# NSA heads: two heads to one float32 transpose, the high and low parts split behind it, and the rotation on VectorE ahead of 1 / rms

## The chip, the cores and the metric

The kernel runs on one core of one Trainium2 chip. The metric is the device time of one execution in microseconds, the median of several runs. The engines are called by the names of the profile: PE (TensorE matmul), PEld (its weight loads), DVE (VectorE), ACT (ScalarE), POOL (GpSimd), SP (SyncE, which only issues transfers).

## The reference, cut to what matters

One layer: a gated feed-forward half step, a mixing part, a second feed-forward half step, and a gated embedding. The change lies in the mixing part, in its native-sparse-attention (NSA) heads. For 512 tokens and 8 query heads, 2 key/value heads of 64 columns:

```
u = a @ w_in                                   # a: normed tokens, 512 x 1024
q_a   = partial_rope(rmsnorm(split_heads(qa, 8), q_norm_nsa), cos, sin)
kc_tok = partial_rope(split_heads(kc, 2), cos, sin)     # compressed keys, no norm
k_slc = partial_rope(rmsnorm(split_heads(ksl, 2), k_norm_slc), cos, sin)
k_win = partial_rope(rmsnorm(split_heads(kwn, 2), k_norm_win), cos, sin)
o_a = nsa_attention(q_a, k_cmp, v_cmp, k_slc, v_slc, k_win, v_win, gates)
```

`rmsnorm` is over the 64 columns of one head, with a gain per column. `partial_rope` rotates the first 16 columns of a head by the token's angle. The rotation and the factor 1 / rms (one number for each token and head) can change places, since a rotation is linear; the gain must stand ahead of the rotation.

## The kernel before, in words

All matrix products are made of float32 split in two parts, hi (the value rounded to the type of TensorE's fast pass, fp32r) and lo (the rest): three passes hi·hi, hi·lo, lo·hi. For the scores of attention a head's 64 columns of hi and 64 of lo stand above each other in the 128 partitions, so that two passes do all.

The program isn't written in the order in which it runs. Every operation is recorded by `Plan.record` (so every instruction has line 306), and `Plan.issue` lists them engine by engine with costs of its own (`Plan.cost`), taking at each step the operation that could start first. So a change in one place moves instructions on all engines. Several streams are woven together by `weave`; the first stage of the mixing part weaves `kv_project` and `q_project(0)` with the compression of keys and values, the second (`c0 n00 | q1`) the attention of the first four heads with `q_project(1)`.

The mixing part lies at 309 to 688 us of the span, the two feed-forward parts on either side of it. What the change touches, each once for each of the four tiles of 128 tokens:

- `c_done` (the projection "c"): scales the columns of the compressed keys and values (tile `u`, a `w` buffer), rotates the two key heads in place with `rope` on POOL, transposes four heads, copies them to `T2`.
- `kv_done` (the projection "v"): four key heads (selected and window, two each). ACT squares, DVE sums (`TENSOR_REDUCE`), POOL makes 1 / rms (`rstd`: two instructions, the tiles `s` and `mhalf`), DVE multiplies by it and then by the gain, POOL rotates (`rope`), ACT and DVE split into hi and lo side by side (`split_heads`, the tile `hl`), PE transposes each head's 128 columns (hi and lo), and ACT or DVE copies three times for each kind into `B`.
- `q_done` (the projections "q0" and "q1"): the same for four query heads, with `head_norm`, and one ACT copy for each two heads (`qT`) into `A`.

`rope` is four instructions: the product with the cosines, two with the sines, and the sum, on 64 columns (four heads) or 32 (two heads). The transposes take PSUM tiles named `gub`; matrix products take `acc` or `gub`. The tiles `st`, `x`, `hi`, `lo` are weights as loaded and as split; each split is an ACT cast to `hi` and a DVE subtraction to `lo`.

Of the kernel before, what the change touches and what calls it, by code (L numbers as in the profile page):

```python
# [7 lines left out]
F32 = mybir.dt.float32  # L8
F32R = mybir.dt.float32r
AF = mybir.ActivationFunctionType  # L10
ALU = mybir.AluOpType
AX = mybir.AxisListType
PSUM = bass.MemoryType.PSUM

P = 128
# [293 lines left out]
class Layer:  # L309
# [443 lines left out]

    def head_norm(self, E, src, dst, gain):
# [31 lines left out]
    def qT(self, hl, heads, dst, t):  # L786

        nc = self.nc
        ps = self.gub()
        for i, hd in enumerate(heads):  # L790
            nc.tensor.transpose(ps[:, i * P:(i + 1) * P], self.parts(hl, hd, 0), self.ident)
        nc.scalar.copy(dst[:, :, t * P:(t + 1) * P], ps[:, :2 * P].rearrange("p (a c) -> p a c", a=2))
# [185 lines left out]
    def cmp_attention(self, A, t, g, o):  # L978
# [4 lines left out]
        for hd in range(4):  # L983
            a = A[hd // 2][:, hd % 2, t * P:(t + 1) * P]
            nc.tensor.matmul(pv[:, hd], lhsT=a, rhs=self.kcT[:, :, g * 32:g * 32 + 32], start=True, stop=True)
# [84 lines left out]
    def mix(self, xT, rs_in, o_nsa, o_fox, nsa_out):  # L1070
# [4 lines left out]
        def c_done(t, ps):  # L1075
# [6 lines left out]
            self.rope(G, uv[:, 0:2], t, 2)  # L1082
# [13 lines left out]
        def kv_project():  # L1096
# [4 lines left out]
            def kv_done(t, ps):  # L1101
                u = self.w2()
                nc.scalar.mul(u, ps, rs_in[t])
                uv = u.rearrange("p (a s h d) -> p a s h d", a=2, s=2, h=2)
                for kind in range(2):
                    self.vsplit(uv[:, kind, 1], Vt[kind], t)
                xn = self.w2()[:, :256]
                x4 = xn.rearrange("p (a h d) -> p a h d", a=2, h=2)
                sq, ss = self.w2()[:, :256], self.small(4)
                nc.scalar.activation(sq.rearrange("p (a h d) -> p a h d", a=2, h=2), uv[:, :, 0], AF.Square)  # L1110
                V.tensor_reduce(ss, sq.rearrange("p (n d) -> p n d", n=4), axis=AX.X, op=ALU.add)
                r = self.rstd(ss, 64, 4).rearrange("p (a h) -> p a h", a=2)
                V.tensor_tensor(x4, uv[:, :, 0], r[:, :, :, None].to_broadcast([P, 2, 2, 64]), ALU.mult)
                V.tensor_tensor(x4, x4, self.gkv[:, :, None, :].to_broadcast([P, 2, 2, 64]), ALU.mult)
                xn = xn.rearrange("p (n d) -> p n d", n=4)
                self.rope(G, xn, t, 4)
                hl = self.split_heads(xn, 4, 2)
                cols = slice(t * P, (t + 1) * P)
                for kind in range(2):
                    tp = self.gub()  # L1120
                    for i in range(2):
                        nc.tensor.transpose(tp[:, i * P:(i + 1) * P], self.parts(hl, 2 * kind + i, 0), self.ident)
                    k = tp[:, :256].rearrange("p (a c) -> p a c", a=2)
                    copy = nc.scalar.copy if (t + kind) % 2 else V.tensor_copy
                    copy(B[kind][0][:, :, cols], k)
                    copy(B[kind][1][0:64, :, cols], k[64:128])
                    copy(B[kind][1][64:128, :, cols], k[0:64])
# [4 lines left out]
        def q_project(g):  # L1132
            A[g] = [self.k4((P, 2, 512), F32R) for _ in range(2)]

            def q_done(t, ps):
# [3 lines left out]
                self.head_norm(V, u, xn, self.gq[:, None, :].to_broadcast([P, 4, 64]))  # L1139
                self.rope(G, xn, t, 4)  # L1140
                hl = self.split_heads(xn, 4, 2)
                for i in range(2):
                    self.qT(hl, (2 * i, 2 * i + 1), A[g][i], t)
# [6 lines left out]
        def nsa_pair(g, a):  # L1150
            for kind in range(2):
# [10 lines left out]
                run = lambda par: self.unit([(A[g][a][:, par], B[kind][i][:, g]) for i in range(2)], Vt[kind][:, g],  # L1162
# [392 lines left out]
```

## Time and profile before

| what | value |
|---|---|
| median of 3 runs | 1085.66 us (1085.31 to 1086.53) |
| the profiled execution: its time | 1086.66 us |
| the profiled execution: its span | 1084.8 us |
| PE busy | 1068.4 us (98%), 6721 matmuls |
| DVE busy | 768.4 us (71%), 1320 instructions |
| ACT busy | 580.2 us (53%) |
| POOL busy | 184.2 us (17%) |
| granted TensorE clock | 1.000 in the mean |
| chain that ended last | PE 86%; DVE 4%; ACT 3%; POOL 3%; DMA 2% |

The span is the time from the first to the last instruction; the execution's own time is 1.9 us longer. A busy engine is one that has an instruction under way; matmuls overlap one another, so PE's busy time tells where PE had something, not what it could have done.

### The profile page before, as it was taken

The numbers are of one execution on the slowest core, as the hardware profiler recorded it, in microseconds if no ns is written. First come the engines' busy times: TensorE is split into PE (matmuls) and PEld (weight loads), VectorE is DVE, ScalarE is ACT, GpSimd is POOL, SyncE is SP. The second block draws the span as 40 slices with busy tenths as digits, with TensorE's granted clock in tenths as the row PEclk, the third lists the DMA queues.
The fourth block names the chain that finished last, engine by engine and source line by source line (L and its number), as shares of the span: only waits on it lengthen the run. The fifth ranks groups of instructions, "written<-read, shape, count | busy, mean of one in ns | idle before, by whom it ended". The sixth has DMA issues, their size and how long they took to land.

```text
span 1084.8 us, 17688 instructions
## 1 busy us (share of the span) xinstructions
PE 1068.4 (98%) x6721; PEld 962.8 (89%) x6721; DVE 768.4 (71%) x1320; ACT 580.2 (53%) x1116; POOL 184.2 (17%) x313
## 2 busy tenths in 40 slices
PE   9999999999999999999999999999999999999998
PEld 6789899988997878999999888889989998899887
DVE  5886378744774777989889786977537784487473
ACT  5544145522543768988888864645315552255352
POOL 0010000000000246554344610310000000000000
PEclk9999999999999999999999999999999999999999
DMA  8396356643444622302102241686535674333421
GB/s 280 125 232 200 97 136 184 189 130 100 118 110 131 216 70 73 86 7 60 43 18 75 76 158 52 220 222 170 173 97 145 185 185 130 103 109 120 153 109 66
DMA packets 76532, 139.79 MB, mean 129 GB/s; under 512 B 13744, under 2 KB 33712, under 8 KB 76192
## 3 DMA queue, kind: packets, MB, share of 16 engines
q1 hardware_dynamic: 71376, 120.76, 34.4%
q0 software_dynamic: 4928, 17.89, 9.4%
q8 instruction: 53, 0.87, 0.3%
q14 instruction: 31, 0.25, 0.1%
q10 hardware_dynamic: 144, 0.02, 0.0%
HBM read 132.23 MB, written 6.42 MB: 128 GB/s over the span
## 4 chain that ended last, share of the span: by engine, by line
PE 86%; DVE 4%; ACT 3%; POOL 3%; DMA 2%; issue 2%; SPq 0%; ACTq 0%; POOLq 0%; DVEq 0%
PE acc L306 53%; PE gub L306 33%; DVE k L306 1%; POOL s L306 1%; DVE lo L306 1%; ACT w L306 1%; DMA st<-in_quarters 1%; DMA st<-in_first 1%; POOL r L306 1%; ACT k L306 1%; POOL w L306 1%; DVE w L306 1%; DMA gq<-in_q_norm_nsa 1%; ACT hi L306 1%; SPq L306 0%
## 5 line engine op out<-in xcount | busy, mean ns | idle before, releaser
L306 PE MATMUL acc<-hi,k 128*128 128x512 f32 (+1 forms) x832 | 262.7, 389 | 1.5 <-ACT k L306 0.9
L306 ACT CAST hi<-st 128x1024 fp32r<-128x1024 f32 (+4 forms) x150 | 148.5, 991 | 179.7 <-PE acc L306 93.2
L306 DVE TENSOR_TENSOR lo<-st,hi 128x1024 fp32r<-128x1024 f32 (+4 forms) x150 | 172.2, 1150 | 65.6 <-ACT hi L306 65.2
L306 PE MATMUL acc<-hi,x 128*128 128x384 f32 (+3 forms) x720 | 199.5, 349 | 0.3 <-ACT hi L306 0.3
L306 PEld LDWEIGHTS acc<-hi,k 128*128 128x128 f32 x832 | 155.9, 188 | 32.6 <-ACT k L306 1.8
L306 PE MATMUL acc<-lo,k 128*128 128x512 f32 (+1 forms) x432 | 163.9, 383 | 0.6 <-DVE lo L306 0.6
L306 ACT CAST hi<-pt 128x1024 fp32r<-128x1024 f32 x68 | 71.4, 1049 | 159.1 <-PE acc L306 90.3
L306 PE MATMUL gub<-x,hi 128*128 128x256 f32 x816 | 147.5, 282 | 0.0
L306 PE MATMUL acc<-x,hi 128*128 128x256 f32 x816 | 147.3, 282 | 0.0
L306 DVE TENSOR_TENSOR lo<-pt,hi 128x1024 fp32r<-128x1024 f32 x68 | 83.2, 1223 | 79.6 <-ACT hi L306 79.6
L306 PE MATMUL gub<-k,hi 128*128 128x512 f32 (+1 forms) x560 | 138.6, 338 | 0.0
L306 PEld LDWEIGHTS acc<-hi,x 128*128 128x128 f32 x720 | 127.2, 189 | 11.0 <-ACT hi L306 0.4
L306 PE MATMUL acc<-lo,x 128*128 128x384 f32 (+3 forms) x360 | 125.0, 348 | 1.7 <-DVE lo L306 1.7
L306 PEld LDWEIGHTS gub<-x,hi 128*128 128x128 f32 x816 | 126.2, 189 | 0.5
L306 PEld LDWEIGHTS acc<-x,hi 128*128 128x128 f32 x816 | 125.7, 189 | 0.0
L306 PE MATMUL gub<-x,lo 128*128 128x256 f32 x408 | 115.3, 283 | 0.0
L306 PE MATMUL acc<-x,lo 128*128 128x256 f32 x408 | 115.3, 283 | 0.0
L306 POOL DMA_DIRECT2D pt<-in_quarters x34 | 29.9, 880 | 476.3 <-DMA pt<-in_quarters 284.8
L306 PEld LDWEIGHTS gub<-k,hi 128*128 128x128 f32 x560 | 96.3, 190 | 12.2 <-ACT hi L306 1.2
L306 PE MATMUL gub<-k,lo 128*128 128x512 f32 (+1 forms) x280 | 94.6, 338 | 0.4 <-DVE lo L306 0.4
L306 PEld LDWEIGHTS acc<-lo,k 128*128 128x128 f32 (+1 forms) x432 | 79.4, 184 | 15.7 <-DVE lo L306 0.9
L306 PEld LDWEIGHTS gub<-x,lo 128*128 128x128 f32 x408 | 76.9, 189 | 0.0
(163 smaller groups left out, 1716.0 us busy)
## 6 DMA issues: line engine op xcount, KB each, us to landing
st<-in_quarters SPq DMA_DIRECT2D x51, 512.0 KB, 3.5
st<-in_ffn_wd SPq DMA_DIRECT2D x44, 512.0 KB, 4.4
pt<-in_quarters SPq DMA_DIRECT2D x34, 512.0 KB, 4.5
pt<-in_quarters POOLq DMA_DIRECT2D x34, 512.0 KB, 6.9
st<-in_quarters SPq DMA_DIRECT2D x32, 256.0 KB, 4.9
st<-in_w_in SPq DMA_DIRECT2D x48, 128.0 KB, 2.3
st<-in_first SPq DMA_DIRECT2D x16, 256.0 KB, 4.0
st<-in_w_in SPq DMA_DIRECT2D x8, 512.0 KB
```

What stands on the lines that cost most here:

```text
L306: getattr(getattr(self.nc, op.eng), m)(*a, **k)
```

## The change

Four things are done at once, in `c_done`, `kv_done` and `q_done`:

- `turned_norm`: the gain comes first, then the rotation, on DVE, and 1 / rms is the last factor. The rotation so stands beside POOL's `rstd` and not behind it.
- `turned`: two heads of 64 float32 columns go into one transpose, so two transposes make a tile of four heads, where four made it before.
- The split into hi and lo is made on the way out of PSUM: ACT copies 64 partitions to hi, DVE subtracts it from the same 64 partitions and writes lo to the other 64.
- `c_done`'s rotation is made by DVE too.

The tiles `A` and `B` are held by other indices (`A[g][par]` for the even or odd heads, `B[g]` for the key/value head); the products that read them are as many and as large.

```diff
+    def turned_norm(self, src, dst, gain, t):
+        V = self.nc.vector
+        d4 = dst.rearrange("p (a h) d -> p a h d", a=2)
+        sq, ss = self.w2()[:, :256], self.small(4)
+        self.nc.scalar.activation(sq.rearrange("p (a h d) -> p a h d", a=2, h=2), src, AF.Square)
+        V.tensor_tensor(d4, src, gain, ALU.mult)
+        V.tensor_reduce(ss, sq.rearrange("p (n d) -> p n d", n=4), axis=AX.X, op=ALU.add)
+        self.rope(V, dst, t, 4)
+        r = self.rstd(ss, 64, 4)
+        V.tensor_tensor(dst, dst, r[:, :, None].to_broadcast([P, 4, 64]), ALU.mult)
...
+    def turned(self, x):
         ps = self.gub()
-        for i, hd in enumerate(heads):
-            nc.tensor.transpose(ps[:, i * P:(i + 1) * P], self.parts(hl, hd, 0), self.ident)
-        nc.scalar.copy(dst[:, :, t * P:(t + 1) * P], ps[:, :2 * P].rearrange("p (a c) -> p a c", a=2))
+        for i in range(2):
+            self.nc.tensor.transpose(ps[:, i * P:(i + 1) * P], x[:, 2 * i:2 * i + 2].rearrange("p a d -> p (a d)"),
+                                     self.ident)
+        return ps[:, :2 * P].rearrange("p (a c) -> p a c", a=2)
+
+    def qT(self, x, dst, t):
+        pv = self.turned(x)
+        for par in range(2):
+            r, o = slice(64 * par, 64 * par + 64), slice(64 - 64 * par, 128 - 64 * par)
+            d = dst[par][:, :, t * P:(t + 1) * P]
+            self.nc.scalar.copy(d[r], pv[r])
+            self.nc.vector.tensor_sub(d[o], pv[r], d[r].bitcast(F32))
@@ c_done @@
-            self.rope(G, uv[:, 0:2], t, 2)
+            self.rope(V, uv[:, 0:2], t, 2)
@@ kv_done @@
-                V.tensor_reduce(ss, sq.rearrange("p (n d) -> p n d", n=4), axis=AX.X, op=ALU.add)
-                r = self.rstd(ss, 64, 4).rearrange("p (a h) -> p a h", a=2)
-                V.tensor_tensor(x4, uv[:, :, 0], r[:, :, :, None].to_broadcast([P, 2, 2, 64]), ALU.mult)
-                V.tensor_tensor(x4, x4, self.gkv[:, :, None, :].to_broadcast([P, 2, 2, 64]), ALU.mult)
-                self.rope(G, xn, t, 4)
-                hl = self.split_heads(xn, 4, 2)
+                self.turned_norm(uv[:, :, 0], xn, self.gkv[:, :, None, :].to_broadcast([P, 2, 2, 64]), t)
+                pv = self.turned(xn)
-                for kind in range(2):
-                    tp = self.gub()
-                    for i in range(2):
-                        nc.tensor.transpose(tp[:, i * P:(i + 1) * P], self.parts(hl, 2 * kind + i, 0), self.ident)
-                    k = tp[:, :256].rearrange("p (a c) -> p a c", a=2)
-                    copy = nc.scalar.copy if (t + kind) % 2 else V.tensor_copy
-                    copy(B[kind][0][:, :, cols], k)
-                    copy(B[kind][1][0:64, :, cols], k[64:128])
-                    copy(B[kind][1][64:128, :, cols], k[0:64])
+                for g in range(2):
+                    r, o = slice(64 * g, 64 * g + 64), slice(64 - 64 * g, 128 - 64 * g)
+                    k = pv[r]
+                    nc.scalar.copy(B[g][0][r, :, cols], k)
+                    V.tensor_sub(B[g][0][o, :, cols], k, B[g][0][r, :, cols].bitcast(F32))
+                    nc.scalar.copy(B[g][1][o, :, cols], k)
+                    V.tensor_sub(B[g][1][r, :, cols], k, B[g][0][r, :, cols].bitcast(F32))
@@ q_done @@
-                self.head_norm(V, u, xn, self.gq[:, None, :].to_broadcast([P, 4, 64]))
-                self.rope(G, xn, t, 4)
-                hl = self.split_heads(xn, 4, 2)
-                for i in range(2):
-                    self.qT(hl, (2 * i, 2 * i + 1), A[g][i], t)
+                self.turned_norm(u.rearrange("p (a h) d -> p a h d", a=2), xn,
+                                 self.gq[:, None, None, :].to_broadcast([P, 2, 2, 64]), t)
+                self.qT(xn, A[g], t)
```

Where the listing puts the instructions, at three places.

PE, in the projection "v", the transposes of the first tile's key heads (`hl` before, `w_641` now, between the matmuls of the second tile). Before:

```order
L306 MATMUL acc<-hi,x_540 128x512
L306 MATMUL acc<-hi,x_538 128x512
L306 MATMUL acc<-lo,x_538 128x512
L306 MATMUL acc<-hi,x_540 128x512
L306 MATMUL acc<-hi,x_538 128x512
L306 MATMUL acc<-lo,x_538 128x512
L306 MATMUL gub<-ident,hl 128x128 x4
L306 MATMUL acc<-hi,x_540 128x512
L306 MATMUL acc<-hi,x_539 128x512
```

PE, the same place in the change:

```order
L306 MATMUL acc<-hi,x_538 128x512
L306 MATMUL acc<-lo,x_538 128x512
L306 MATMUL acc<-hi,x_540 128x512
L306 MATMUL gub<-ident,w_641 128x128 x2
L306 MATMUL acc<-hi,x_538 128x512
L306 MATMUL acc<-lo,x_538 128x512
L306 MATMUL acc<-hi,x_540 128x512
L306 MATMUL acc<-hi,x_538 128x512
L306 MATMUL acc<-lo,x_538 128x512
```

Four transposes became two, and they stand five matmuls of 512 columns earlier (row 1960 of the engine's list, where it was 1965).

POOL, where the query tiles of the first group are normed (`w_714`, `w_728`, `w_739` are the first three tiles before; `s_742`, `s_755` are 1 / rms of the third and fourth). Before:

```order
L306 TENSOR_TENSOR r_718<-w_714,cos 128x64
L306 TENSOR_TENSOR r_719<-w_714,sin 128x4x8 x2
L306 TENSOR_TENSOR w_714<-r_718,r_719 128x4x16
L306 TENSOR_SCALAR s_742<-s_741 128x4
L306 TENSOR_TENSOR s_742<-s_742,mhalf 128x4
L306 TENSOR_TENSOR r_732<-w_728,cos 128x64
L306 TENSOR_TENSOR r_733<-w_728,sin 128x4x8 x2
L306 MEMSET k_773 128x1024
L306 TENSOR_TENSOR w_728<-r_732,r_733 128x4x16
L306 TENSOR_SCALAR s_755<-s_754 128x4
L306 TENSOR_TENSOR r_743<-w_739,cos 128x64
L306 TENSOR_TENSOR r_744<-w_739,sin 128x4x8 x2
```

POOL, the same place in the change (`s_723`, `s_732`, `s_743` are 1 / rms of the second, third and fourth tile):

```order
L306 MEMSET k_757 128x1024
L306 TENSOR_SCALAR s_723<-s_720 128x4
L306 TENSOR_TENSOR s_723<-s_723,mhalf 128x4
L306 TENSOR_SCALAR s_732<-s_729 128x4
L306 TENSOR_TENSOR s_732<-s_732,mhalf 128x4
L306 TENSOR_SCALAR s_743<-s_740 128x4
L306 TENSOR_TENSOR s_743<-s_743,mhalf 128x4
L306 TENSOR_TENSOR pt<-pt 128x8 x3
```

POOL's rotations are gone from between the tiles' 1 / rms.

DVE, where the weights of the projection "q0" are split (`lo<-st`), beside the last key tiles (`w_667` is the third tile before, `w_663` now). Before:

```order
L306 TENSOR_TENSOR lo<-x_626,hi 128x1024
L306 TENSOR_REDUCE s_669<-w_668 128x4
L306 TENSOR_TENSOR lo<-x_627,hi 128x1024 x2
L306 TENSOR_TENSOR w_667<-w_666,s_670 128x256
L306 TENSOR_TENSOR lo<-st,hi 128x1024
L306 TENSOR_TENSOR w_667<-w_667,gkv 128x256
```

DVE, the same place in the change:

```order
L306 TENSOR_TENSOR r_667<-w_663,sin 128x4x8 x2
L306 TENSOR_TENSOR w_663<-r_666,r_667 128x4x16
L306 TENSOR_TENSOR lo<-x_626,hi 128x1024 x2
L306 TENSOR_TENSOR k_613<-gub,k_612 64x2x128
L306 TENSOR_TENSOR lo<-x_627,hi 128x1024
L306 TENSOR_REDUCE s_665<-w_664 128x4
L306 TENSOR_TENSOR lo<-x_627,hi 128x1024
L306 TENSOR_TENSOR lo<-st,hi 128x1024
L306 TENSOR_TENSOR w_663<-w_663,s_668 128x256
```

The product with 1 / rms (`w_663<-w_663,s_668`), which waits for POOL, now stands behind the split of the weights and not ahead of it; the rotation and a subtraction out of PSUM stand ahead.

Counted over the whole program, PE has 24 matmuls fewer (the transposes), DVE 72 instructions more (64 of them the rotations), ACT 8 fewer, and POOL 64 fewer.

## Rows read from the trace of the kernel before

**Rows 1.** Busy time of each engine by stretch of the mixing part.
```profile
core 0: us, PE busy (x) PEld busy (x) DVE busy (x) ACT busy (x) POOL busy (x), PEclk, DMA share, GB/s
370.00:450.00 80.00, 74.53 (x510) 66.40 (x510) 65.12 (x166) 62.50 (x152) 44.01 (x90) 1.00 0.25 72
450.00:490.00 40.00, 40.00 (x276) 37.72 (x275) 34.94 (x113) 33.79 (x102) 19.15 (x35) 1.00 0.17 42
490.00:610.00 120.00, 119.22 (x782) 110.99 (x781) 105.94 (x302) 102.98 (x291) 53.27 (x78) 1.00 0.17 45
```
**Rows 2.** Chain that ended last, 385 to 407 us: start, us, what.
```profile
385.38 0.57 POOL s L306
386.02 1.17 POOL s L306
387.21 0.44 DVE w L306
387.67 0.44 DVE w L306
388.18 0.81 POOL r L306 x3
389.06 0.33 POOL w L306
389.41 0.41 ACT hl L306
389.85 0.44 DVE hl L306
...
406.57 1.24 POOL w L306
```
**Rows 3.** Timeline of PE: start, us, instruction, idle time before and releaser.
```profile
376.93 0.63 PE L306 MATMUL gub<-ident,w 128*64 128x128 f32 x4 [0.44 <-POOL w L306]
...
390.33 0.66 PE L306 MATMUL gub<-ident,hl 128*128 128x128 f32 x4 [1.14 <-DVE hl L306]
...
405.33 0.38 PE L306 MATMUL acc<-lo,x 128*128 128x256 f32 x1 [1.10 <-DVE lo L306]
...
412.89 0.45 PE L306 MATMUL acc<-lo,k 128*64 128x256 f32 x2 [0.56 <-DVE lo L306]
...
427.70 0.66 PE L306 MATMUL gub<-ident,hl 128*128 128x128 f32 x4 [0.39 <-DVE hl L306]
```
**Rows 4.** Timeline of PE around one tile's four transposes, 395 to 397 us.
```profile
395.47 0.40 PE L306 MATMUL acc<-lo,x 128*128 128x512 f32 x1
395.70 0.39 PE L306 MATMUL acc<-hi,x 128*128 128x512 f32 x1
395.94 0.60 PE L306 MATMUL gub<-ident,hl 128*128 128x128 f32 x4
396.29 0.48 PE L306 MATMUL acc<-hi,x 128*128 128x512 f32 x1
396.61 0.39 PE L306 MATMUL acc<-lo,x 128*128 128x512 f32 x1
```
**Rows 5.** POOL's groups, 360 to 490 us: count, busy us, mean ns, idle before.
```profile
L306 POOL TENSOR_TENSOR r<-w,cos 128x64 f32<-128x64 f32 x12 | 6.4, 530 | 8.0 <-DVE w L306 7.9
L306 POOL TENSOR_TENSOR r<-w,sin 128x32 f32<-128x32 f32 x24 | 6.3, 283 | 0.0
L306 POOL TENSOR_TENSOR w<-r,r 128x64 f32<-128x64 f32 x12 | 5.6, 468 | 0.8
```
**Rows 6.** DVE's group of the split, 366 to 490 us, columns as above.
```profile
L306 DVE TENSOR_TENSOR hl<-w,hl 128x256 fp32r<-128x256 f32 x14 | 5.9, 424 | 4.8 <-ACT hl L306 4.6
```
**Rows 7.** Timeline of DVE, columns as in the timeline of PE.
```profile
390.80 1.29 DVE L306 CAST k<-gub 128x256 fp32r<-128x256 f32 x3 [0.20 <-PE gub L306]
...
403.71 0.42 DVE L306 TENSOR_TENSOR w<-w,s 128x256 f32<-128x256 f32 x1 [0.91 <-POOL s L306]
404.05 1.22 DVE L306 TENSOR_TENSOR lo<-st,hi 128x1024 fp32r<-128x1024 f32 x1
...
427.56 0.17 DVE L306 TENSOR_SCALAR w<-ch 128x32 f32<-128x32 f32 x1
427.64 0.17 DVE L306 TENSOR_SCALAR w<-pt 128x32 f32<-128x32 f32 x1
```
**Rows 8.** ACT's group of the split, 366 to 490 us.
```profile
L306 ACT CAST hl<-w 128x256 fp32r<-128x256 f32 x14 | 5.8, 412 | 4.7 <-POOL w L306 4.7
```

More of the change, by code (lines that the diff above doesn't have):

```diff
@@ L784, in parts @@
         return hl[:, hd, i:i + 2].rearrange("p a d -> p (a d)").bitcast(F32)
-    def qT(self, hl, heads, dst, t):
-        nc = self.nc
+    def turned(self, x):
         ps = self.gub()
-        for i, hd in enumerate(heads):
-            nc.tensor.transpose(ps[:, i * P:(i + 1) * P], self.parts(hl, hd, 0), self.ident)
-        nc.scalar.copy(dst[:, :, t * P:(t + 1) * P], ps[:, :2 * P].rearrange("p (a c) -> p a c", a=2))
+        for i in range(2):
[9 more added lines that the diff above has]
+            self.nc.vector.tensor_sub(d[o], pv[r], d[r].bitcast(F32))
     def vsplit(self, src, dst, t):
@@ L983, in cmp_attention @@
         for hd in range(4):
-            a = A[hd // 2][:, hd % 2, t * P:(t + 1) * P]
+            a = A[hd % 2][:, hd // 2, t * P:(t + 1) * P]
             nc.tensor.matmul(pv[:, hd], lhsT=a, rhs=self.kcT[:, :, g * 32:g * 32 + 32], start=True, stop=True)
@@ L1106, in kv_done @@
                     self.vsplit(uv[:, kind, 1], Vt[kind], t)
[L1107 to L1110, printed above, removed]
-                V.tensor_reduce(ss, sq.rearrange("p (n d) -> p n d", n=4), axis=AX.X, op=ALU.add)
-                r = self.rstd(ss, 64, 4).rearrange("p (a h) -> p a h", a=2)
-                V.tensor_tensor(x4, uv[:, :, 0], r[:, :, :, None].to_broadcast([P, 2, 2, 64]), ALU.mult)
-                V.tensor_tensor(x4, x4, self.gkv[:, :, None, :].to_broadcast([P, 2, 2, 64]), ALU.mult)
-                xn = xn.rearrange("p (n d) -> p n d", n=4)
-                self.rope(G, xn, t, 4)
-                hl = self.split_heads(xn, 4, 2)
-                cols = slice(t * P, (t + 1) * P)
-                for kind in range(2):
-                    tp = self.gub()
-                    for i in range(2):
-                        nc.tensor.transpose(tp[:, i * P:(i + 1) * P], self.parts(hl, 2 * kind + i, 0), self.ident)
-                    k = tp[:, :256].rearrange("p (a c) -> p a c", a=2)
-                    copy = nc.scalar.copy if (t + kind) % 2 else V.tensor_copy
-                    copy(B[kind][0][:, :, cols], k)
-                    copy(B[kind][1][0:64, :, cols], k[64:128])
-                    copy(B[kind][1][64:128, :, cols], k[0:64])
+                xn = self.w2()[:, :256].rearrange("p (n d) -> p n d", n=4)
+                self.turned_norm(uv[:, :, 0], xn, self.gkv[:, :, None, :].to_broadcast([P, 2, 2, 64]), t)
+                pv = self.turned(xn)
+                cols = slice(t * P, (t + 1) * P)
+                for g in range(2):
[5 more added lines that the diff above has]
+                    V.tensor_sub(B[g][1][r, :, cols], k, B[g][0][r, :, cols].bitcast(F32))
             yield from self.project(xT, [(768, 512)], kv_done, "v")
@@ L1161, in write @@
                                     tmp.rearrange("p (t c) -> p t c", t=NT), ALU.add)
-                run = lambda par: self.unit([(A[g][a][:, par], B[kind][i][:, g]) for i in range(2)], Vt[kind][:, g],
+                run = lambda par: self.unit([(A[g][par][:, a], B[g][i][:, kind]) for i in range(2)], Vt[kind][:, g],
                                             rs, par)
```

## The prediction

> **What bounds the kernel now.** I read the page first: PE is busy nearly all of the span, and the chain that ended last is PE's for 86% of it. Then I cut the mixing part into stretches, because the change lies in the first two [rows 1]. From 370 to 450 us, where the key heads and the first four query heads are projected and normed, PE is busy 74.53 of 80 us: it waits for 5.47 us. From 450 to 490 us, where the other query heads are made beside the first attention, PE is busy all the time and DVE 34.94 of 40 us. So in the second stretch PE's work itself sets the time, and in the first PE's work and a chain through the other engines in turn.
>
> The chain of one key tile shows what that chain is [rows 2]. POOL makes 1 / rms from 385.38 to 387.19 us, DVE multiplies twice, POOL rotates from 388.18 to 389.39, ACT splits off hi, DVE lo, and PE's transposes start at 390.33 [rows 3]. Between the end of POOL's 1 / rms and the transposes lie 3.1 us. PE waited 1.14 us for the last link, 0.44 us for a rotation in `c_done`, 0.39 us for the split of a query tile; and twice, 1.10 and 0.56 us, for DVE's split of weights (`lo`) [rows 3]. These five are 3.6 of the 5.47 us; the rest is in small pieces.
>
> **PE's own work.** Twelve tiles (four of keys, eight of queries) lose two transposes each, 24 in all. Price: from the matmul at 395.70 to the one at 396.61 there pass 0.91 us, in which two matmuls of 512 columns and four transposes start [rows 4]. A matmul of 512 columns takes 0.23 us start to start (395.47 to 395.70). So four transposes take 0.91 - 0.46 = 0.45 us, one 0.11, and 24 take 2.6 us. Eight of the 24 (0.9 us) lie in the second group's projection, where PE never waits; the other 16 (1.8 us) lie where PE also waits, so they count in full only if the chain gets shorter too. The matmuls that read `A` and `B` are the same in number and size, and cost the same.
>
> **The chain.** With the change 1 / rms is followed by one product (0.44 us) and the transposes. The second product, from 387.67 to 388.11 us, and what stands from there to 390.33, the rotation and both splits, fall out of it: 0.44 + 2.22 = 2.66 us for each tile. The rotation on DVE must fit beside POOL's 1.81 us of 1 / rms; by the price below it does. The first tile's transposes stand five matmuls earlier in PE's list, which takes 5 x 0.23 = 1.2 us of the 2.66 back; 1.5 us is left, over the wait of 1.14, so I let that wait go. I let go the 0.44 (POOL's rotation is not there any more, and the listing sets those transposes ten matmuls later) and the 0.39. Of the waits for weights I take 0.5 of 1.66 us away: the split that PE waits for at 405.33 started at 404.05 behind a product that had waited 0.91 us for POOL [rows 7]; that product now stands behind the split. Together 2.5 us less of waiting.
>
> **DVE, which pays.** The rotations: no row has one on DVE. From above: each instruction starts when the one ahead has ended. 32 columns last 0.17 us and 256 columns 0.42 [rows 7]; in between by the line, 64 columns 0.21 and 16 columns 0.15; so 0.21 + 0.17 + 0.17 + 0.21 = 0.76 us for four heads and 0.64 for two. From below: they start as soon as DVE takes them, 0.08 us apart at 32 columns (427.56, 427.64) and 0.34 at 256 (403.71, 404.05), so 0.12 at 64 and 0.06 at 16; 0.40 and 0.28 us. I take 0.6 and 0.5, between the two, since the three products don't wait for each other and the sum does. Twelve and four of them: 9.2 us (5.9 to 11.7). The evacuations: 32 subtractions out of PSUM come, twelve copies out of PSUM and twelve splits go. Three such copies took 1.29 us, 0.43 each [rows 7], a split 0.42 [rows 6]: 13.8 - 5.2 - 5.0 = 3.6 us. DVE so gains 12.8 us of work (9.5 to 15.3): 2.0 in `c_done`, 2.5 with the keys, 4.1 with each group of queries. The stretch to 450 us has 14.9 us in which DVE is idle and takes 8.6 of it; the stretch to 490 us has 5.1 us and takes 4.1 [rows 1]. It fits, but in the second stretch DVE is then busy 39 of 40 us, and its instructions stand in one line with the softmax. For that I set 1.0 us of new waiting for PE, between nothing (all of it fits) and 4.1 us (every added microsecond is passed on).
>
> A rule of the Trainium skill (VectorE: DVE Perf Modes, section "Two Vector instructions with no wait between them") speaks against the change: an instruction whose input or output starts in another group of 32 partitions than the last one in the same memory is held until all earlier ones have finished. The copies at 390.80, which go to the other half of the partitions, bear it out: 0.43 us each, where the product at 403.71 gave way after 0.34. By the rule each of the 32 subtractions also holds what follows it, 0.09 us more each, so 2.9 us more of DVE work than the sum has; with the crowding grown in proportion, 1.2 for 1.0 us, the time would be 1081.8.
>
> **ACT and POOL.** ACT loses twelve splits of 0.41 us [rows 8], 4.9 us, and gets a few narrow copies for wide ones; it was busy 62.5 of 80 us and on the path only within the chain counted above, so this is worth nothing more. POOL loses twelve rotations of 0.53 + 2 x 0.28 + 0.47 = 1.56 us [rows 5], 18.7 us, and those of `c_done`. It was busy 44 of 80 us, so as work that is worth nothing; as delay it is, because the sum of one rotation took 0.33 us at 389.06 and 1.24 us at 406.57 [rows 2], and POOL's 1 / rms stands in one line with it. I leave that in the rival of the larger gain. No transfer is added or moved past another; after 490 us nothing is changed but the places in the list.
>
> **Sum.** -2.6 (transposes) - 2.5 (waits gone) + 1.0 (DVE crowded) = -4.1 us. The profiled execution took 1086.66 us and would take 1082.6; it lies 1.0 us over the median of the runs shown, which stands for what will be measured: 1085.66 - 4.1 = **1081.6 us**. The likeliest case reaches from 1079.4 (no crowding, and the rest of the waits for weights, 1.2 us, gone too) to 1083.4 (2.8 us of crowding).
>
> **Rivals.**
> *DVE becomes the bound (slower).* The place is 404 to 490 us, the two query projections, where softmax, splits of weights and the new subtractions share DVE. If half of the 12.8 us that DVE gains is passed on to PE, that is +6.4 - 2.6 = +3.8 us: 1089.5. It decides from 2.6 + 2.5 = 5.1 us passed on. For it: 87% busy DVE in the second stretch already, 88% in the third. Against it: DVE's idle time in the first stretch is in part waits that the change takes away (4.6 us before the splits [rows 6]).
> *The transposes were covered.* If PE goes on waiting in the first stretch, for weights and other tiles, the 16 transposes there save nothing, and only 8 x 0.11 = 0.9 us is left: 1084.8, no change. For it: the second and third longest waits are for weights [rows 3], which DVE now makes behind more work. Against it: PE is busy 93% there, so most transposes did take time.
> *All the first stretch's waiting goes.* With POOL free of rotations and each query tile 2.7 us sooner, the attention can fill what is left: 5.47 + 2.6 = 8.1 us less: 1077.6. For it: ACT stood idle 4.7 us for POOL's rotations ahead of the splits [rows 8]. Against it: waits for transferred and split weights have nothing to do with the change.
> A listing that comes out worse elsewhere, by a new wait of some 1 us as those in [rows 3], is part of each case's width.
>
> **How the numbers follow.** A measurement of this kernel can tell about 0.2%, 2.2 us, from no change: below 1083.5 is faster, above 1087.8 slower. Chances: the forecast 0.48, all waits gone 0.15, covered 0.20, DVE the bound 0.17. So faster 0.48 + 0.15 = 0.63, same 0.20, slower 0.17. The range holds all but the slower case: 1077 to 1087.
>
> **What would show it.** Right: PE's transposes in the projections "v", "q0", "q1" two to a tile, no wait of PE for a split of heads, DVE some 10 to 15 us busier up to 490 us, PE idle 2 to 4 us in 370 to 450. Wrong: PE waiting for DVE's `lo` or for the softmax's tiles for over 5 us up to 490 us (then DVE is the bound); PE idle still over 5 us before 450 (covered); rotations on DVE over 0.8 us each.

## The result, and the profile after

The changed kernel takes 1092.65 us (median of 4 runs, 1091.36 to 1094.81); the kernel before, run beside it, 1085.49 us (1084.64 to 1086.53). The ratio is 1.0069, with an interval of 1.0057 to 1.0081: the change makes the kernel 7 us slower, where 4.1 us less was forecast. The profiled execution took 1092.93 us with a span of 1091.2 us.

The first part of the page after, with the busy time of each engine:

```profile
span 1091.2 us, 17622 instructions
PE 1070.9 (98%) x6697; PEld 963.7 (88%) x6697; DVE 780.4 (72%) x1392; ACT 579.7 (53%) x1108; POOL 161.1 (15%) x249
```

PE's 24 instructions are gone, and DVE's added work is 780.4 - 768.4 = 12.0 us, where 12.8 was forecast. But PE is busy 2.5 us longer, not 2.6 us less. The view by stretch says why (the columns are those of [rows 1]; after the five busy times comes the granted clock):

```profile
370.00:450.00 80.00, 70.42 (x461) 62.73 (x460) 67.01 (x196) 57.24 (x130) 27.34 (x40) 0.96 0.25 72
450.00:490.00 40.00, 38.89 (x255) 34.75 (x253) 38.99 (x128) 30.46 (x91) 13.29 (x24) 1.00 0.17 41
...
32.00:36.00 4.00, 4.00 (x12) 3.10 (x12) 4.00 (x7) 3.03 (x5) 0.00 (x0) 0.58 0.85 257
...
390.00:394.00 4.00, 4.00 (x12) 3.13 (x11) 3.20 (x11) 1.45 (x4) 1.21 (x2) 0.57 0.01 4
...
430.00:436.00 6.00, 4.14 (x23) 3.94 (x23) 5.78 (x18) 2.28 (x7) 1.92 (x4) 0.72 0.00 0
...
431.86:436.00 4.14, 4.14 (x23) 3.94 (x23) 3.98 (x13) 1.54 (x5) 1.92 (x4) 0.66 0.00 0
```

In 370 to 450 us PE now stands idle 9.58 us, where it was 5.47 [rows 1], and the granted clock is 0.96, where it was 1.00. The short stretches show where: from 390 to 394 us and from 430 to 436 us the clock lies part of the time at the lower of its two levels, 1.2 GHz for 2.4. PE is busy all through the first, and from 431.86 us on in the second, so (1 - 0.57) x 4 + (1 - 0.66) x 4.14 = 3.1 us of work at full speed are lost there, and 1.7 us by the same fall at 32 to 36 us, far ahead of the change.

So the 6.4 us between the two spans are: half speed +4.8 us, idle time of PE +3.9 us (1091.2 - 1070.9 = 20.3, for 1084.8 - 1068.4 = 16.4), and PE's work -2.3 us (1070.9 - 4.8 = 1066.1, for 1068.4). Two spans can be set beside each other only roughly. PE's list is the same in all kernels of this document up to its 2253rd matmul, and their profiles reach that matmul at 363.2 to 367.4 us, with nothing changed ahead of it. Here it starts at 366.41 us before and at 366.09 after: the fall at 32 to 36 us is made up for by then, and the whole loss lies behind.

The waits of 370 to 700 us (engine, tile, what it waits for: us in total, times, longest) and PE's timeline name the idle time:

```profile
PE gub L306 <- DVE k L306: 3.9, 3, 3.0
PE gub L306 <- DVE w L306: 3.3, 3, 2.4
PE acc L306 <- DVE lo L306: 2.3, 3, 1.9
```

```profile
389.51 0.44 PE L306 MATMUL gub<-ident,w 128*128 128x128 f32 x2 [2.43 <-DVE w L306]
...
390.25 0.98 PE L306 MATMUL acc<-hi,x 128*128 128x512 f32 x2
391.03 0.63 PE L306 MATMUL acc<-lo,x 128*128 128x512 f32 x1
391.46 1.05 PE L306 MATMUL acc<-hi,x 128*128 128x512 f32 x2
...
429.50 0.41 PE L306 MATMUL gub<-ident,w 128*128 128x128 f32 x2 [2.97 <-DVE k L306]
431.86 0.58 PE L306 MATMUL acc<-lo,x 128*128 128x256 f32 x1 [1.95 <-DVE lo L306]
```

The first key tile's transposes wait 2.43 us for the last product, where the wait for the split was 1.14 [rows 3]; two more waits of 3.0 and 1.95 us come with a query tile. Behind 389.51 a matmul of 512 columns takes 0.43 us start to start (391.03 to 391.46), where it took 0.23 [rows 4].

Why the first key tile is late, by the timeline of DVE and POOL:

```profile
379.36 0.42 DVE L306 COPY k<-gub 64x256 f32<-64x256 f32 x1 [1.43 <-ACT k L306]
...
381.36 3.79 POOL L306 TENSOR_TENSOR k<-k,pos 128x496 f32<-128x496 f32 x2 [16.59 <-DVE k L306]
...
382.25 1.75 DVE L306 TENSOR_TENSOR k<-k,k 128x512 fp32r<-128x512 f32 x1
383.92 1.51 DVE L306 TENSOR_TENSOR w<-w,gkv 128x256 f32<-128x256 f32 x1
...
385.36 1.28 DVE L306 TENSOR_TENSOR k<-k,k 128x512 fp32r<-128x512 f32 x2
386.56 0.41 DVE L306 TENSOR_REDUCE s<-w 128x4 f32<-128x256 f32 x1
...
387.06 0.70 POOL L306 TENSOR_SCALAR s<-s 128x4 f32<-128x4 f32 x1 [1.91 <-DVE s L306]
...
389.03 0.43 DVE L306 TENSOR_TENSOR w<-w,s 128x256 f32<-128x256 f32 x1 [0.46 <-POOL s L306]
389.37 0.42 DVE L306 TENSOR_TENSOR w<-w,gkv 128x256 f32<-128x256 f32 x1
```

POOL's 1 / rms starts at 387.06 us, where it started at 385.38 [rows 2]: 1.68 us later. Ahead of it the reduction stands behind the gain's product, which took 1.51 us beside POOL's 3.79 us of `k<-k,pos` and only 0.42 us at 389.37, without POOL. The Trainium skill (SBUF — State Buffer, section "Who interferes with whom") says that a VectorE instruction with two inputs in SBUF contends with a GpSimd instruction that reads SBUF; the 1.51 and 0.42 us agree, and so do the products `k<-k,k`, 1.75 us for one beside POOL and 1.28 us for two once POOL had ended at 385.15 us.

On the query tile the new way out of PSUM shows. The timeline of ACT and DVE around its bank:

```profile
426.91 0.43 DVE L306 TENSOR_TENSOR w<-w,s 128x256 f32<-128x256 f32 x1 [1.18 <-POOL s L306]
...
427.83 0.42 DVE L306 TENSOR_TENSOR k<-gub,k 64x256 fp32r<-64x256 f32 x1
...
428.28 0.37 ACT L306 CAST k<-gub 64x256 fp32r<-64x256 f32 x1 [1.47 <-DVE k L306]
...
428.93 0.43 DVE L306 TENSOR_TENSOR k<-gub,k 64x256 fp32r<-64x256 f32 x1
```

ACT's second copy waits for DVE's first subtraction on the same bank, and that stood behind a product that had waited 1.18 us for POOL. The next tile's transposes, whose data was ready at 427.34 us (426.91 + 0.43), start at 429.50, behind the subtraction's end (428.93 + 0.43): the wait of 2.97 us is put down to it, `DVE k`.

### The profile page after: what moved, and what is told of

Its sections match the earlier page's. It is cut to its first block, busy times and chain, and to the rows that moved or that the text cites. A ratio compares the mean times of both kernels' runs of the same rounds, so it can differ in the third digit from the quotient of the medians.

```text
span 1091.2 us, 17622 instructions
## 1 busy us (share of the span) xinstructions
PE 1070.9 (98%) x6697; PEld 963.7 (88%) x6697; DVE 780.4 (72%) x1392; ACT 579.7 (53%) x1108; POOL 161.1 (15%) x249
## 4 chain that ended last, share of the span: by engine, by line
PE 88%; DVE 5%; ACT 2%; POOL 2%; DMA 2%; issue 1%; SPq 0%; ACTq 0%; DVEq 0%; POOLq 0%
PE acc L306 54%; PE gub L306 34%; DVE k L306 1%; POOL s L306 1%; DVE lo L306 1%; DVE w L306 1%; ACT w L306 1%; DMA st<-in_quarters 1%; DMA st<-in_first 1%; ACT k L306 1%; DVE s L306 0%; POOL w L306 0%; SPq L306 0%; ACT hi L306 0%; DVE pt L306 0%
## 5 line engine op out<-in xcount | busy, mean ns | idle before, releaser
L306 PE MATMUL acc<-hi,x 128*128 128x384 f32 (+3 forms) x720 | 203.0, 354 | 0.5 <-ACT hi L306 0.5
L306 PEld LDWEIGHTS acc<-x,lo 128*128 128x128 f32 x408 | 76.9, 188 | 0.0
```

Of the source, the lines that this page charges most:

```text
L306: getattr(getattr(self.nc, op.eng), m)(*a, **k)
```

## The experiments

Every kernel was timed beside the kernel before (medians 1085.15 to 1085.54 us). Idle is the profiled span less PE's busy time on the page; the clock is that of 370 to 450 us.

| kernel | median us | ratio, interval | span | PE busy | idle | clock |
|---|---|---|---|---|---|---|
| before | | | 1084.8 | 1068.4 | 16.4 | 1.00 |
| changed | 1092.65 | 1.0069 (1.0057 to 1.0081) | 1091.2 | 1070.9 | 20.3 | 0.96 |
| norm_only | 1092.63 | 1.0065 (1.0053 to 1.0077) | 1089.8 | 1073.3 | 16.5 | 0.91 |
| evac_only | 1090.96 | 1.0058 (1.0043 to 1.0073) | 1088.3 | 1068.5 | 19.8 | 0.94 |
| rope_pool | 1091.63 | 1.0055 (1.0042 to 1.0067) | 1089.6 | 1071.4 | 18.2 | 0.94 |
| batch | 1088.97 | 1.0040 (1.0029 to 1.0052) | 1089.4 | 1069.3 | 20.1 | 0.94 |
| late1000 | 1091.06 | 1.0054 (1.0042 to 1.0067) | 1090.6 | 1070.3 | 20.3 | 0.96 |
| late2000 | 1091.13 | 1.0055 (1.0042 to 1.0068) | 1089.4 | 1071.9 | 17.5 | 0.91 |
| batch_late2000 | 1091.03 | 1.0058 (1.0046 to 1.0071) | 1092.6 | 1072.8 | 19.8 | 0.98 |
| before_early | 1096.13 | 1.0094 (1.0078 to 1.0109) | 1096.2 | 1073.4 | 22.8 | 0.96 |
| norm_fill | 1088.74 | 1.0032 (1.0020 to 1.0044) | 1085.7 | 1072.7 | 13.0 | 0.98 |
| evac_fill | 1086.90 | 1.0014 (1.0006 to 1.0023) | 1085.4 | 1071.9 | 13.5 | 1.00 |
| batch_fill | 1087.14 | 1.0020 (1.0011 to 1.0029) | 1085.6 | 1071.4 | 14.2 | 0.98 |
| before_gap | 1088.14 | 1.0028 (1.0016 to 1.0040) | 1090.1 | 1071.8 | 18.3 | 0.96 |
| after_fill | 1089.37 | 1.0032 (1.0019 to 1.0045) | 1088.0 | 1074.2 | 13.8 | 1.00 |
| late2000_fill | 1089.63 | 1.0035 (1.0022 to 1.0049) | 1088.4 | 1073.4 | 15.0 | 1.00 |
| evac_late2000 | 1081.91 | 0.9968 (0.9955 to 0.9980) | 1078.8 | 1065.7 | 13.1 | 1.00 |
| evac_late3000 | 1084.84 | 1.0001 (0.9990 to 1.0012) | 1085.2 | 1069.2 | 16.0 | 1.00 |
| before_late1000 | 1088.15 | 1.0020 (1.0010 to 1.0030) | 1084.4 | 1069.9 | 14.5 | 0.98 |
| before_late2000 | 1090.12 | 1.0038 (1.0024 to 1.0053) | 1085.8 | 1069.5 | 16.3 | 1.00 |

### Which part costs the time

The first theories: A, the copies and subtractions that take turns on a bank; B, the rotations' work on DVE; C, only the new places in the list.

**norm_only**: the kernel before with `turned_norm` and `c_done`'s rotation on DVE; four transposes to a tile, as before.

```diff
-                self.head_norm(V, u, xn, self.gq[:, None, :].to_broadcast([P, 4, 64]))
-                self.rope(G, xn, t, 4)
+                self.turned_norm(u.rearrange("p (a h) d -> p a h d", a=2), xn,
+                                 self.gq[:, None, None, :].to_broadcast([P, 2, 2, 64]), t)
```

> The norm part of the change alone: gain, then rotation on VectorE, 1 / rms last, and c_done's rotation on VectorE; split_heads, the four transposes and the old copies out of PSUM stay as before. Theory A (the new evacuation is the loss: ScalarE's copies and VectorE's subtractions take turns on one PSUM bank, and each turn stands in VectorE's line): this is not slower than before, 1082 to 1087 us. Theory B (VectorE's rotations are the loss, 9 us of work on a full engine): most of the 7 us is here, 1089 to 1092. Theory C (only the new places in the list, any edit costs a few us): anything from 1084 to 1093, and no pattern over these four runs.

**evac_only**: the changed kernel with the old order of the normalization and all rotations on POOL.

```diff
-        V.tensor_tensor(d4, src, gain, ALU.mult)
...
-        V.tensor_tensor(dst, dst, r[:, :, None].to_broadcast([P, 4, 64]), ALU.mult)
+        V.tensor_tensor(d4, src, r[:, :, :, None].to_broadcast([P, 2, 2, 64]), ALU.mult)
+        V.tensor_tensor(d4, d4, gain, ALU.mult)
+        self.rope(self.nc.gpsimd, dst, t, 4)
```

> The other part alone: two heads to a float32 transpose and the split on the way out of PSUM; the norm in its old order with both rotations on GpSimd. Theory A: most of the 7 us is here, 1089 to 1093 us. Theory B: about before less the 24 transposes, 1082 to 1086. Theory C: no pattern.

**rope_pool**: the changed kernel with `rope(G, ...)` for `rope(V, ...)` in both places, the new order kept.

> The change with its rotations (also c_done's) back on GpSimd; the new order of the norm and the new evacuation stay. Theory A: 1089 to 1094 us, as the change. Theory B: VectorE loses some 9 us of work, 1083 to 1088. Theory C: no pattern.

**batch**: the changed kernel, ACT's copies out of a bank all ahead of DVE's subtractions.

```diff
             self.nc.scalar.copy(d[r], pv[r])
+        for par in range(2):
+            r, o = slice(64 * par, 64 * par + 64), slice(64 - 64 * par, 128 - 64 * par)
+            d = dst[par][:, :, t * P:(t + 1) * P]
             self.nc.vector.tensor_sub(d[o], pv[r], d[r].bitcast(F32))
```

> The change with ScalarE's copies out of a PSUM tile all ahead of VectorE's subtractions from it, so that the bank passes from one engine to the other once and not three or seven times; the same instructions. Theory A: the tile of PSUM is free 1 to 2 us sooner and the time falls by 3 us or more, to 1084 to 1089. Theory B: no change, 1091 to 1094. Theory C: no pattern.

Measured: each half alone costs as much as both (1.0065 and 1.0058 for 1.0069), the rotations back on POOL give nothing back that can be told, and batch gives back some 3 us. So B fell, and no sum of parts explains the whole. A's ranges hold the last three kernels but not norm_only (1092.63, where A had at most 1087). Nor is A's mechanism shown: in batch's profile the wait for `DVE k` is gone, but PE is idle 20.1 us for 20.3, and like the other three this edit moves the list too, so C stands. What the slow kernels had in common was in the last column, and norm_only shows it best: it stands idle 16.5 us, as the kernel before does, and has the same matmuls; nearly all that it loses it loses while PE is busy.

### The places in the list

**late1000, late2000**: the changed kernel; the planner's latency from the last product to TensorE is raised, so that the transposes are listed later.

```diff
-        V.tensor_tensor(dst, dst, r[:, :, None].to_broadcast([P, 4, 64]), ALU.mult)
+        V.tensor_tensor(dst, dst, r[:, :, None].to_broadcast([P, 4, 64]), ALU.mult).lat = dict(
+            Plan.LAT["vector"], tensor=255.0 + 2000.0)
```

> Theory D: after's instructions are good ones, but the planner's costs place the transposes of the key and query tiles on TensorE before the chip has served them; the waits of 2.4 to 3.0 us that come of it (389.51, 429.50 and 431.86 us in after) cost their own time and, since the granted clock falls to the lower level behind each, as much again. Here the instructions are after's and only the planner's latency from the last product of the normalization to TensorE is 1 us longer, so that the first key tile's transposes stand about five matmuls later. D: about half of the first wait goes, longest wait in 370 to 450 us near 1.5 to 2.5 us, 1087 to 1090. Rival A (the copies and subtractions that alternate on one bank of PSUM) and B (the work of the rotations on VectorE): nothing of theirs changes, 1091 to 1094.

> After's instructions, planner's latency from the last product to TensorE 2 us longer; the first key tile's transposes stand some nine matmuls later than in after, about as long as TensorE waited for them. D: no wait above 1.3 us on the first key tile, granted clock near 1.0 in 370 to 450 us, 1082 to 1087, which is the time before or below it. Were the waits only moved to later places (A, B): still 1089 to 1094 with waits of over 2 us on the query tiles.

**batch_late2000**: batch with the same latency.

> As the run before, with ScalarE's copies of a tile ahead of VectorE's subtractions besides, as in the run batch (1088.97). If the alternation on a bank and the place in the list are two causes that add (D with A): 2 to 4 us below the run with the latency alone, 1079 to 1084. If the place alone decides (D): within 1.5 us of it, 1082 to 1086. If neither: 1087 to 1090, as batch.

**before_early**: the kernel before, `tensor=255.0 - 1500.0` at the subtraction of `split_heads`.

> The kernel before with its own instructions; only the planner's latency from VectorE's low half of a head split to TensorE is 1.5 us shorter, so that the transposes of the split stand earlier in TensorE's list. D: the waits on the key and query tiles grow to 2 us and more, the granted clock falls behind them, and the time is 1088 to 1092 although no instruction is other than before. A and B: nothing that they name is in this kernel, 1084 to 1087.

before_early came out at 1096.13 us with the instructions of before, 4 us above D's range: places alone can cost 11 us. But theory D in its simple form fell: late1000 and late2000 lie above its ranges, and batch_late2000 (1091.03) above all three of its own, so with the later list batch's gain is gone. late2000's profile is idle only 1.1 us more than that of before, with no wait over 1.8 us, and it still takes 1091.13. Its clock is 0.91. So the clock was tried by itself.

### The clock

Theory E: what costs is less the wait than the fall of the clock behind it. F: the clock is a by-product. **norm_fill, evac_fill, batch_fill**: the runs above, with transposes of the identity that nothing reads, put in PE's list where PE had waited (numbers are places in that list).

```diff
+    FILL = {2377: 20, 2603: 15}
...
+            if op.eng == "tensor":
+                pe += 1
+                for _ in range(self.FILL.get(pe, 0)):
+                    self.nc.tensor.transpose(a[0], self.ident[:], self.ident[:])
```

> The run norm_only with 35 transposes of the identity added in TensorE's list, 20 ahead of the first key tile's transposes and 15 ahead of the first query tile's, into the bank that those write next; they compute nothing that is kept, and everything else is as in norm_only (1092.63), which waited 2.3 and 1.8 us at these two places and ran 13.6 us at the lower clock behind them. Theory E (the waits cost little themselves; what costs is that the granted clock falls behind them): TensorE is busy during the waits, the clock stays at 1.0 in 370 to 450 us, and the time falls by 4 to 5 us to 1087 to 1089, although work is added. Rival F (the time is in the waits and in what is late behind them; the clock is a by-product): 1092 to 1094.

> The run evac_only (1090.96) with 60 such transposes ahead of three tiles' own, 12, 16 and 32 for waits of 1.4, 2.0 and 3.7 us. E: no fall of the clock in 370 to 450 us, 1086.5 to 1088.5. F: 1090.5 to 1092.5.

> The run batch (1088.97) with 41 such transposes, 21, 4 and 16 ahead of tiles whose transposes waited 2.4, 0.6 and 1.9 us. E: the clock stays up and 2.5 to 3.5 us come back, 1085.5 to 1087, no slower than the kernel before within 0.2%. F: 1088.5 to 1090.

Added work made all three faster: 3.9, 4.1 and 1.8 us. The first two lie in E's ranges, batch_fill 0.1 us above its own. Two stretches of norm_only, and then norm_fill's:

```profile
388.00:394.00 6.00, 4.69 (x16) 3.90 (x17) 4.33 (x15) 2.43 (x7) 1.21 (x2) 0.72 0.00 0
426.00:438.00 12.00, 11.40 (x59) 10.64 (x60) 8.75 (x33) 8.79 (x23) 5.21 (x6) 0.57 0.01 1
```

```profile
388.00:394.00 6.00, 5.97 (x30) 4.73 (x29) 4.50 (x14) 3.97 (x11) 1.21 (x2) 1.00 0.00 0
426.00:438.00 12.00, 10.64 (x77) 9.94 (x75) 8.96 (x35) 9.38 (x25) 3.11 (x5) 0.86 0.15 36
```

And the added transposes in PE's timeline of norm_fill, with the tile's own right behind them:

```profile
385.34 2.35 PE L312 MATMUL gub<-ident 128*128 128x128 f32 x20
387.78 0.66 PE L313 MATMUL gub<-ident,hl 128*128 128x128 f32 x4
```

In norm_only (1 - 0.72) x 6 + (1 - 0.57) x 12 = 6.8 us are lost at most; with the fill, 0.12 us each, the first fall is gone and the second is 1.7 us. It isn't one execution's luck: the mean clock of the whole span, on record for every execution, is 0.993 in all five of norm_only and 0.997 or 0.998 in all six of norm_fill, and 0.0045 of 1090 us is 4.9 us. This is E's result; by F no time would come back.

**before_gap** is the other direction: the kernel before, the first key tile's transposes ahead of the nine matmuls that stood just ahead of them.

```diff
+                if 2368 <= pe < 2377:
+                    held.append(op)
+                    continue
...
+            if pe == 2380 and op.eng == "tensor":
+                for h in held:
+                    getattr(self.nc.tensor, h.call[0])(*h.call[1], **h.call[2])
```

> The kernel before with one change in TensorE's list: the first key tile's four transposes stand ahead of the nine matmuls that stood just ahead of them, so that the wait at 390.33 us grows from 1.1 to some 3.2 us. The matmuls are the same and come behind. E: the clock falls to 0.5 for a few us behind this one wait; 2.1 us of waiting and 1.7 us of half speed, 1088.5 to 1090. F: at most the longer wait, 1085.5 to 1087.5, and clock 1.0.

The timeline of PE in before_gap, and the stretch behind the wait:

```profile
387.06 0.39 PE L314 MATMUL acc<-lo,x 128*128 128x512 f32 x1
390.64 1.12 PE L314 MATMUL gub<-ident,hl 128*128 128x128 f32 x4 [3.20 <-DVE hl L314]
```

```profile
390.00:396.00 6.00, 5.36 (x15) 4.40 (x16) 2.87 (x7) 1.55 (x5) 2.28 (x6) 0.50 0.01 3
```

One wait of 3.2 us, for 1.14, and the clock is 0.50 over the next 6 us, in which PE is busy 5.36: 2.7 us lost, more than the 2.1 us of the longer wait. But this is the slowest of nine executions, from 1085.1 to 1091.98 us, and the median, 1088.14, lies between the two ranges. The mean clock of each tells them apart: the four at 0.999 or 1.000 take 1085.1 to 1087.0 us, which is F's range, the longer wait alone; the five at 0.995 to 0.998 take 1088.1 to 1092.0. The kernel before does the same: of its 81 executions beside the experiments ten are at 0.997 or 0.998, with a median of 1087.5 us, and the others at 1085.2. So in one and the same kernel a lower clock and a longer time go together, and the fall comes in some executions and not in others.

**after_fill, late2000_fill**: the changed kernel and late2000 with such a fill, in part repeats of a matmul into unused columns.

> The changed kernel with 59 instructions added on TensorE whose results nothing reads: 21 transposes of the identity where it waited 2.4 us (389.51 us), 24 repeats of a 256-column matmul where it waited 3.0 us (429.50) and 14 where it waited 1.9 us (431.86). E (the clock is the cause): no fall of the granted clock in 370 to 450 us, the 3.4 us of half speed seen in the one profile go: 1087 to 1089.5. F (the waits and what comes late behind them): 1092 to 1094.

> The run late2000 (1091.13), which waited little more than the kernel before but ran 13.7 us at the lower clock, with 45 such instructions at the five places where it waited 0.6 to 1.8 us. E: clock 1.0 in 400 to 440 us and 4 to 6 us back: 1085 to 1087, the time before within 0.2%, since the saving of the transposes is eaten by the waits that stay. F: 1090.5 to 1092.5.

The clock is 1.00 in both. after_fill came out as E had it, 3.3 us below the changed kernel. So the clock is something like half of the changed kernel's 7 us; the waits themselves, which a fill only covers, are the rest. late2000_fill is a miss: 1.5 us back for 4 to 6, between E's range and F's. Its 45 added instructions take some 5 us at 0.12 each, while idle time fell by 2.5 us only (15.0 for 17.5); a fill can hold the clock, but gives nothing else back.

### The waits filled with the kernel's own matmuls

**evac_late2000, evac_late3000**: evac_only; the latency from the rotation's last sum on POOL to TensorE raised by 2 and 3 us.

```diff
-        E.tensor_tensor(x[:, :, 0:16], r[:, :n], q[:, :n], ALU.add)
+        E.tensor_tensor(x[:, :, 0:16], r[:, :n], q[:, :n], ALU.add).lat = dict(
+            self.nc.LAT["gpsimd" if E is self.nc.gpsimd else "vector"], **({"tensor": 150.0 + 2000.0} if E is self.nc.gpsimd else {}))
```

> The run evac_only (rotations on GpSimd, two transposes to a tile) with the planner's latency from the rotation's last sum on GpSimd to TensorE 2 us longer, so that the transposes stand 13 to 72 places later among the kernel's own matmuls. E: if the waits of 1.4, 2.0 and 3.7 us go with it, the clock stays up and the transposes' 2.6 us are saved, 1081.5 to 1084.5, faster than both kernels; if new waits of 2 us come up for weights, the clock falls behind those and it is 1087 to 1091. F: 1087 to 1090.

> As the run before with 3 us. E: the same two cases, 1081.5 to 1084.5 with the clock at 1.0 throughout 370 to 450 us, 1087 to 1091 where it falls. F: 1087 to 1090.

evac_late2000 takes 1081.91 us, faster than both kernels. The first lines of its page and of its stretches, and its longest waits in 370 to 450 us:

```profile
PE 1065.7 (99%) x6697; PEld 960.2 (89%) x6697; DVE 771.8 (72%) x1328; ACT 578.7 (54%) x1108; POOL 183.0 (17%) x313
```

```profile
370.00:450.00 80.00, 75.19 (x502) 66.04 (x502) 69.33 (x172) 64.50 (x153) 46.53 (x90) 1.00 0.28 78
```

```profile
PE acc L306 <- DVE lo L306: 2.3, 4, 0.9
PE gub L306 <- DVE k L306: 0.7, 1, 0.7
```

No wait is over 0.9 us, the clock stays up, and PE has 1068.4 - 1065.7 = 2.7 us less to do, which is what the 24 transposes were to save. (Of the profile's 6.0 us 2.6 lie ahead of the 2253rd matmul, which starts at 363.78 us for 366.41 and ahead of which nothing was changed; the ratio, some 3.5 us, is the size to use.) With 3 us the same kernel takes 1084.84 us, as long as before and just above E's 1084.5. So 2 us is the better of two tries, and the list decides over as much as the change.

**before_late1000, before_late2000** tell whether the listing alone gains.

```diff
-        nc.vector.tensor_sub(hl[:, :, 1], src, hl[:, :, 0].bitcast(F32))
+        nc.vector.tensor_sub(hl[:, :, 1], src, hl[:, :, 0].bitcast(F32)).lat = dict(
+            Plan.LAT["vector"], tensor=255.0 + 1000.0)
```

> The kernel before with the planner's latency from VectorE's low half of a head split to TensorE 1 us longer, so that the transposes stand later in TensorE's list. If the gain of evac_late2000 is the 24 transposes that it does without: 1084 to 1086.5, since only the 1.1 us wait at 390.33 can go. If the later listing is what gains: 1081.5 to 1083.5.

> As the run before with 2 us, the same latency as in evac_late2000. Transposes: 1084 to 1087. Listing: 1081 to 1083. A fall of the clock behind a wait that the new list makes would add some 2 us and more to either and shows in the granted clock.

It doesn't: 1088.15 and 1090.12, slower than before and than either theory had it. So the gain of evac_late2000 isn't to be had by these latencies alone. The profiled execution of before_late2000 was the fastest of its six (1087.53, mean clock 0.999) and shows no fall. The slowest (1092.28) is at 0.996, which is 3.3 of the 4.8 us between the two; why even the fastest is 2 us above before isn't shown.

## Why the prediction was wrong, point by point

- **PE's own work: right, as far as it can be told.** -2.6 us was forecast; evac_late2000, with the same matmuls and the clock at 1.00, has 2.7 us less, and the changed kernel 2.3 once half speed is taken off. That they agree so well is in part luck: evac_late3000 has the same matmuls and PE is busy 1069.2 us, of which only 1.5 are lost by a fall of the clock at 31 to 35 us, and before_late2000, with the matmuls of before and no fall, has 1069.5.
- **DVE's work: right.** 12.0 us for 12.8. The groups of DVE, 366 to 490 us:

```profile
L306 DVE TENSOR_TENSOR k<-gub,k 64x256 fp32r<-64x256 f32 x32 | 13.5, 421 | 3.2 <-ACT k L306 2.4
L306 DVE TENSOR_TENSOR r<-w,sin 128x32 f32<-128x32 f32 x24 | 3.9, 198 | 0.1
L306 DVE TENSOR_TENSOR w<-r,r 128x64 f32<-128x64 f32 x12 | 2.6, 219 | 0.2
L306 DVE TENSOR_TENSOR r<-w,cos 128x64 f32<-128x64 f32 x12 | 2.6, 216 | 0.1
```

  A rotation of four heads is (3.9 + 2.6 + 2.6) / 12 = 0.76 us, the upper bound and not the 0.6 taken; the subtractions are 0.42 us each, as taken. What stands behind a subtraction does start 0.45 us after it (428.28 behind 427.83, 429.38 behind 428.93) and not 0.34, as the rule in the prediction has it; the total still stayed below the sum.
- **The crowding of 450 to 490 us: right, with luck.** DVE is busy 38.99 of 40 us and PE waits 1.1 us, for 39 and 1.0. But the changed kernel is late by then, and the stretch holds 255 matmuls where it held 276, so it isn't the same work.
- **The chain: the step that failed.** It is the sum's term of -2.5 us, waits gone: PE's idle time in 370 to 450 us rose by 4.1 us instead (9.58 for 5.47). It broke at the first key tile: "The first tile's transposes stand five matmuls earlier in PE's list, which takes 5 x 0.23 = 1.2 us of the 2.66 back; 1.5 us is left, over the wait of 1.14, so I let that wait go." The 2.66 us took for granted that 1 / rms starts when it did. It starts 1.68 us later. 1.36 of these come from `c_done`: its last transposes are listed ten matmuls later, the copy into `T2` is at 379.36 us, where the kernel before has it at 378.00 (below), and DVE's and POOL's products on `T2` follow. The prediction named those ten places and priced them only as a wait that goes. Nor would the old places have served: the rotation's sum on DVE stands behind a split of weights of 1.22 us and ends at 377.92 us, where POOL's ended at 376.88, a delay for which the prediction had no term. The rest of the 1.68 us comes from the gain's product, now ahead of the reduction. So the product ends only 0.8 us earlier than the split did, and PE comes 2.1 us earlier, not 1.2 (387.08 for 389.19, idle start of both rows). Of that difference 0.44 us is the wait in `c_done`, which did go: PE, let go there, stands at the next place the longer. 1.14 - 0.8 + 2.1 = 2.4 us, the wait seen. The timelines of POOL and DVE before, then those of DVE and PE after:

```profile
376.63 0.25 POOL L306 TENSOR_TENSOR w<-r,r 128x32 f32<-128x32 f32 x1
378.00 0.42 DVE L306 COPY k<-gub 64x256 f32<-64x256 f32 x1
```

```profile
376.61 1.22 DVE L306 TENSOR_TENSOR lo<-st,hi 128x1024 fp32r<-128x1024 f32 x1
377.74 0.18 DVE L306 TENSOR_TENSOR w<-r,r 128x32 f32<-128x32 f32 x1
378.32 0.60 PE L306 MATMUL gub<-ident,w 128*64 128x128 f32 x4
```

- **What had no term.** The way out of PSUM in four turns of ACT and DVE on one bank, behind which the wait of 2.97 us stands; what it costs isn't shown apart from the places in the list, since batch is some 3 us faster than the change and batch_late2000 no faster than late2000. And the clock, which the sum left at 1.00: 3.1 us of the profiled execution behind the change, 3.3 us by after_fill, and nearly all of norm_only's loss.
- **The rivals.** "DVE becomes the bound" had the sign, and 1089.5 us for 1092.65, but not the mechanism: DVE is busy 67 of 80 us in the slow stretch, and taking the rotations off it (rope_pool) gave nothing. What was late were single instructions in DVE's line, not its work. "The transposes were covered" had its sign come true, PE idle over 5 us before 450, but no loss in it.
- **Open.** late2000 and evac_late2000 differ in the order of the normalization and in the rotations' engine, and lie 9.2 us apart, their profiles 10.6. Of these 4.4 us are idle time (17.5 for 13.1) and 6.2 are PE's busy time, which half speed, at most (1 - 0.91) x 80 = 7 us, covers; which of the two differences makes the places so much better isn't shown. Nor is it shown what decides whether a given wait costs the clock.

## What to carry to other kernels

Where one engine is busy 98% of the time and its order is fixed by a list, price a change by where its operations land in that list as well as by what they take, and follow every piece that the list moves later, not only those that it moves earlier. A wait of TensorE (here 2 to 3 us) may be charged twice, once as idle time and again at half speed behind it; look at the granted clock by short stretches, and test it by putting throwaway matmuls into the wait. If that helps, move the kernel's own matmuls there: in the better of two tries that turned the +6 us of evac_only into -3.5.

## What the runs showed of the hardware

The granted clock fell to the lower level behind waits of 2 to 3 us in a program that is otherwise 98% busy, and stayed there when PE was busy again (0.50 over 390 to 396 us in before_gap). It isn't certain to, and the length of the wait doesn't tell. In late2000 it stayed at 1.00 behind a wait of 1.81 us and fell behind one of 1.59 us; PE's timeline and the stretches:

```profile
395.84 0.39 PE L306 MATMUL acc<-hi,k 128*128 128x256 f32 x1 [1.81 <-ACT hi L306]
404.74 0.39 PE L306 MATMUL acc<-lo,x 128*128 128x256 f32 x1 [1.59 <-DVE lo L306]
```

```profile
394.00:399.00 5.00, 3.19 (x19) 2.67 (x19) 4.88 (x12) 4.88 (x11) 0.00 (x0) 1.00 0.00 0
404.00:409.00 5.00, 4.26 (x23) 4.26 (x24) 4.23 (x12) 4.71 (x8) 2.94 (x3) 0.66 0.74 219
```

Ahead of the change nothing was touched, and there too the profiles of the two kernels differ; the stretches of before, and then those of the changed kernel:

```profile
28.00:32.00 4.00, 1.57 (x7) 0.84 (x7) 2.06 (x4) 3.81 (x5) 1.49 (x4) 1.00 0.11 43
32.00:36.00 4.00, 4.00 (x19) 3.31 (x18) 4.00 (x6) 3.02 (x5) 0.00 (x0) 1.00 0.76 207
```

```profile
28.00:32.00 4.00, 2.07 (x10) 1.27 (x9) 2.43 (x3) 3.87 (x6) 0.74 (x2) 0.99 0.11 39
```

Before, PE was busy 1.57 of 4 us and the clock behind was 1.00; after, it was busy 2.07 of the same 4 us and the clock behind was 0.58. The Trainium skill (TensorE: Matmul & The Clock Gate, section "What's actually happening") says that the engine's default is the lower clock and that activity releases it; the runs with a fill agree.
